# A two-layer mixer and expert kernel: the framework orders the engines' instructions by its time line simulation, and operands are put at equal places

## The chip, the core and the metric

The kernel runs on one core of a Trainium2 chip. The metric is the device time of one execution in microseconds. Five engines work side by side, each through its own list of instructions, strictly in the list's order: PE multiplies matrices (PEld is its loading of the stationary operand), DVE and ACT do elementwise work, POOL does small work and indirect DMAs, SP issues most of the DMAs. An instruction that has to wait for a semaphore holds up everything behind it on its engine.

## The reference

Two layers over 1,024 tokens of width 1,024 and 256 context tokens. In each layer:

```
h_x, h_c = modulate(x, ...), modulate(ctx, ...)          # layer norm, then scale and shift from w_mod
y_x, y_c = token_mixer(h_x, h_c, ...)                    # 4 mLSTM heads both ways and 4 attention heads, then w_out
x = post_norm(x, mx[2] * y_x, ln1_g, ln1_b)
x = post_norm(x, mx[5] * ec_moe(modulate(x, ...), w_router, w_gate, w_up, w_down), ln2_g, ln2_b)
```

`ec_moe` lets each of 16 experts take its 128 best tokens (32 of the context), multiplies them by `w_gate`, `w_up` and `w_down` (1024x1024 each) and adds the results back to their rows. Layer 0 does the same for the context; layer 1 has no context output.

## The kernel before

Float32 products are made from three fast matmuls (`mm3`, L83): an operand is split into a rounded part (`hi_act`, ACT, L90) and the rest (`lo_dve`, DVE, L93).

```
mm(ps, lh, rh, start=start, stop=False)     # L85: the first operand stays in the array,
mm(ps, lh, rl, start=False, stop=False)     # L86: the second streams through it
mm(ps, ll, rh, start=False, stop=stop)      # L87
```

The stages of a layer, with their time in layer 0 and layer 1 in the profile:

- Input (`phase_in`, L1492; 0 to 480 and 1795 to 2240 us). The normed and transposed input is held as `hTh0..2` and `hTl0..2` (`make_hT` L257, `border_hT` L289). Each of four mLSTM heads (`mlstm_head`, L551) projects K, V, Q and O (`p_block`, L339), convolves, and then goes through its chunks of 128 tokens: small matmuls that alternate with ACT, DVE and POOL. The transposed output of a head (`mlstm_out`, L664, whose transposes are L670 and read `hb`) is traced late, in the middle of the next head (`run_late`, L676), so that two streams lie side by side on PE: the next head's projections and this head's chunks.
- Attention (`latents` L681, `prep_kv` L790, `phase_mla` L809; 480 to 830 and 2240 to 2500 us).
- Output projection, norms, router (`phase_out`, L1006; 830 to 1040 and 2500 to 2640 us): ten tiles of 128 tokens in layer 0, eight in layer 1, each 48 matmuls of `omh`/`oml` with `woh`/`wol`; then the choice of tokens (`topk`, L1182), a serial chain on DVE.
- Experts (`phase_moe`, L1271; 1040 to 1795 and 2675 to 3245 us). `wsplit` (L1292) loads 512 KB of weights into a ring, splits it (`mhi`, `mlo`) and feeds PE: per expert 96 matmuls for gate and up (`A_ps`, operands `xTh`/`xTl`) and 48 for down (`B_ps`, operands `aTh`/`aTl`), each 128x512. Results are added to `zd` by indirect DMA (L1268). At the end of layer 0, layer 1 loads `w_in` (L336) and the rows of `zd` (`nz`, L1525).

What sets the order of the work: the Python code is traced in program order through a tile framework. When its context closes, the framework decides in which order the instructions of each engine stand in the program, places the tiles in SBUF and sets the semaphores. In the kernel before this order comes from a priority list: an earlier traced instruction has the higher priority, and a later one goes ahead of it where the framework takes the earlier one not to be ready yet. So the order isn't the traced one; for example the L670 transposes stand between the matmuls of a projection. One order is asked for by hand: the first four `lo_dve` of the experts stand behind the last row norm (L1301).

Tiles of a pool lie one behind the other in each partition, pools are stacked from the left and from the right. By the program's allocation, in bytes of a partition:

| matmuls | one operand | the other | apart, of 128 bytes |
|---|---|---|---|
| gate/up, both layers | xTh 131,040 | mhi 151,520 | 0 |
| down, layer 0 | aTh 64,832 | mhi 151,520 | 32 |
| down, layer 1 | aTh 47,520 | mhi 151,520 | 64 |
| output projection, layer 0 | omh 68,224 | woh 131,040 | 32 |
| output projection, layer 1 | omh 60,896 | woh 131,040 | 0 |
| scores (L763 to L767) | qh 45,728 | knh 128,992 | 64 |
| input, layer 0, `hTl0` with `whi` | hTl0 188,320 | whi 126,816 | 64 |

(`hTh2` and `hTl2` have 258 columns, 8,256 bytes, in layer 0, which is 64 more than a multiple of 128.) `hi` and `lo` parts lie alike.

Of the kernel before, what the change touches and what calls it, by code (L numbers as in the profile page):

```python
# [9 lines left out]
F32 = mybir.dt.float32  # L10
# [41 lines left out]
class Kern:  # L52
# [21 lines left out]
    def pool(self, es, name, bufs=1, space=None, side=None):  # L74
        kw = {"reuse_waits": "tile"}
        if space is not None:
            kw["space"] = space
        if side is not None:
            kw["side"] = side
        return es.enter_context(self.tc.tile_pool(name=name, bufs=bufs, **kw))  # L80


    def mm3(self, ps, lh, ll, rh, rl, start, stop):  # L83
# [173 lines left out]
    def make_hT(self, l, xrows, hp, p, psum, tag, ready, done):  # L257

        nc = self.nc
        cols = [n + 2 * (self.fold and g == 2) for g, (_, n) in enumerate(GROUPS)]  # L260
        self.hTh = [hp.tile([128, 8, n], F32R, name=f"hTh{g}") for g, n in enumerate(cols)]
        self.hTl = [hp.tile([128, 8, n], F32R, name=f"hTl{g}") for g, n in enumerate(cols)]

        def normed(i):
            xt = xrows(i)
            self.layer_norm_rows(xt, xt, 1e-6, p)
            return xt

        for g, (t0, n) in enumerate(GROUPS):
            hh, hl = self.hTh[g], self.hTl[g]  # L270
            xn = []
            for i in range(t0 // 128, (t0 + n) // 128):
                xn.append(normed(i))
                if g:
                    self.fill(self.nfill[0])
            if g == 0:
                ready()
            s = 1 if g == 2 else 0
            for kb in range(8):
                pt = psum.tile([128, 512], F32, name="pt", tag=tag)  # L280
                for i, xo in enumerate(xn):
                    nc.tensor.transpose(pt[:, i * 128:(i + 1) * 128], xo[:, kb * 128:(kb + 1) * 128], self.ident)
                sc = self.modc[l][:, s, 1, kb:kb + 1]
                nc.scalar.activation(hh[:, kb, :n], pt[:, :n], AF.Copy, scale=sc)
                nc.vector.scalar_tensor_tensor(hl[:, kb, :n], pt[:, :n], sc, hh[:, kb, :n].bitcast(F32), op0=OP.mult,
                                               op1=OP.subtract)
            done(g)
# [502 lines left out]
    def prep_kv(self, l, p2):  # L790

        nc, A = self.nc, self.A
        wkh = p2.tile([128, 2, 8, 128], F32R, name="wkh")
        wkl = p2.tile([128, 2, 8, 128], F32R, name="wkl")
        ckh = p2.tile([128, 2, TT], F32R, name="ckh")
        ckl = p2.tile([128, 2, TT], F32R, name="ckl")
        for kb in range(2):
            raw = p2.tile([128, 1024], F32, name="araw", tag="araw", bufs=1)
            nc.sync.dma_start(raw, A["w_ukv"][l, kb * 128:(kb + 1) * 128, :])
            rv = raw.rearrange("p (h w c) -> p w h c", h=4, w=2)  # L800
            hv = wkh[:, kb].rearrange("p (w h) c -> p w h c", w=2)
            lv = wkl[:, kb].rearrange("p (w h) c -> p w h c", w=2)
            for w in range(2):
                self.hi_act(hv[:, w], rv[:, w])
                self.lo_dve(lv[:, w], rv[:, w], hv[:, w])
        self.kv = p2, (wkh, wkl, ckh, ckl)
        yield from self.rms_norm_T(l, 1, 2, 55, (0, 1, 2), ckh, ckl, p2)

    def phase_mla(self, l, ctx_out, el):  # L809
# [3 lines left out]
        with ExitStack() as es:  # L813
# [49 lines left out]
                self.lo_dve(Vl[:, c, :], ps, Vh[:, c, :])  # L863
            el.close()
            pa = self.pool(es, f"aa{l}")
            rope = {}

            def project_q(ps, blk, t0, n):
# [84 lines left out]
            def stage(n, k):  # L953

                if n >= len(pairs):
                    return
                g, h, i0 = pairs[n]
                if k == 0 and i0 == 0:
                    if h % 2 == 0:
                        prep_rope(g, h // 2)  # L960
                    qs[g, h] = prep_q(g, h)
                elif k == 1:
                    ps_[n] = weights(g, h, i0, qs[g, h])
# [2 lines left out]
                stage(n, 0)  # L966
            for n in range(1):
                stage(n, 1)
            for n, (g, h, i0) in enumerate(pairs):
                stage(n + 2, 0)  # L970
                stage(n + 1, 1)
                if i0 == 0:
                    aos[g, h] = pa.tile([128, 512], F32, name="ao", tag="ao", bufs=2)
                ao = aos[g, h]
                values(g, h, i0, ps_.pop(n), ao)
                t0, nn = GROUPS[g]
                if i0 + 2 == nn // 128:
                    nc.scalar.dma_start(self.mixd[l][512 + h * 128:512 + (h + 1) * 128, t0:t0 + nn], ao[:, :nn])
# [27 lines left out]
    def phase_out(self, l, ctx_out, xsrc, es_keep):  # L1006
# [14 lines left out]
        self.sel = {}  # L1021
        with ExitStack() as es:
            p = self.pool(es, f"om{l}")
            n_tiles = NCH if ctx_out else NXC
            mixes = {}

# [244 lines left out]
    def phase_moe(self, l, ctx_out):  # L1271
# [2 lines left out]
        psum, tkp = self.psum, self.tkp  # L1274
        with ExitStack() as es:
            p = self.pool(es, f"mm{l}")
            md = self.modd[l]
            g5 = self.row(p, "g5", md[0:1, 5 * D:6 * D])
            if ctx_out:
# [359 lines left out]
```

## Time and profile before

| | us |
|---|---|
| three runs | 3304.8, 3297.15, 3305.44 |
| median | 3304.8 |
| the profiled execution: own time | 3297.7 |
| its span (first to last instruction) | 3295.6 |
| PE busy in the span | 3081.4 |
| DVE, ACT busy | 2373.5, 1790.0 |

How to read it: the views below are of that one profiled execution. Busy time of PE is not PE at its peak, as matmuls overlap; the distance from one start to the next tells the pace. "Idle before" names what ended a wait, and PEclk is the granted share of TensorE's clock, 1.0 for 2.4 GHz and 0.5 for 1.2 GHz.

### The profile page before, as it was taken

The numbers are of one execution on the slowest core, as the hardware profiler recorded it, in microseconds if no ns is written. First come the engines' busy times: TensorE is split into PE (matmuls) and PEld (weight loads), VectorE is DVE, ScalarE is ACT, GpSimd is POOL, SyncE is SP. The second block draws the span as 40 slices with busy tenths as digits, with TensorE's granted clock in tenths as the row PEclk, the third lists the DMA queues.
The fourth block names the chain that finished last, engine by engine and source line by source line (L and its number), as shares of the span: only waits on it lengthen the run. The fifth ranks groups of instructions, "written<-read, shape, count | busy, mean of one in ns | idle before, by whom it ended". The sixth has DMA issues, their size and how long they took to land.

```text
span 3295.6 us, 49911 instructions
## 1 busy us (share of the span) xinstructions
PE 3081.4 (94%) x18387; PEld 2405.8 (73%) x18387; DVE 2373.5 (72%) x4350; ACT 1790.0 (54%) x3057; POOL 392.7 (12%) x301
## 2 busy tenths in 40 slices
PE   7999999999998999999997799998998869999997
PEld 4667777788775777777775677786887758777775
DVE  5556655666677878777776676646776779999897
ACT  2323334455324666666664743334553358888786
POOL 0001001000010011011101201000000113343111
PEclk8999999999998999999999899999999979999999
DMA  6654213101658887788786332223015479999995
GB/s 229 200 161 120 66 63 90 37 25 61 226 198 311 303 291 281 291 300 293 285 297 208 108 89 77 65 85 80 20 39 195 144 273 383 384 376 383 355 359 180
DMA packets 259405, 653.82 MB, mean 198 GB/s; under 512 B 29430, under 2 KB 99128, under 8 KB 259160
## 3 DMA queue, kind: packets, MB, share of 16 engines
q1 hardware_dynamic: 234616, 581.03, 49.2%
q0 software_dynamic: 12592, 39.85, 5.0%
q10 hardware_dynamic: 11952, 29.76, 2.4%
q8 instruction: 144, 2.36, 0.3%
q14 instruction: 101, 0.83, 0.1%
HBM read 580.45 MB, written 62.75 MB: 195 GB/s over the span
## 4 chain that ended last, share of the span: by engine, by line
PE 60%; DVE 6%; DMA 3%; ACT 2%; issue 2%; POOL 1%; SPq 0%; POOLq 0%; ACTq 0%; DVEq 0%
PE A_ps L86 11%; PE A_ps L85 10%; PE A_ps L87 10%; PE C_ps L1328 5%; PE B_ps L86 3%; PE B_ps L87 3%; PE B_ps L85 3%; PE D_ps L1316 1%; PE C_ps L1122 1%; DMA E<-mxd 1%; PE B_ps L935 1%; DVE mlo L93 1%; PE D_ps L85 1%; PE B_ps L593 1%; PE D_ps L86 1%
## 5 line engine op out<-in xcount | busy, mean ns | idle before, releaser
L93 DVE TENSOR_TENSOR mlo<-mraw,mhi 128x1024 fp32r<-128x1024 f32 x768 | 911.2, 1221 | 148.5 <-ACT mhi L90 130.8
L90 ACT ACTIVATE mhi<-mraw 128x1024 fp32r<-128x1024 f32 x768 | 803.8, 1064 | 238.1 <-PE A_ps L87 148.0
L86 PE MATMUL A_ps<-mlo,xTh 128*128 128x512 f32 x1024 | 411.1, 401 | 7.8 <-DVE mlo L93 7.5
L87 PE MATMUL A_ps<-mhi,xTl 128*128 128x512 f32 x1024 | 404.2, 395 | 0.0
L85 PE MATMUL A_ps<-mhi,xTh 128*128 128x512 f32 x1024 | 396.0, 401 | 0.0
L85 PE MATMUL A_ps<-hTh,whi 128*128 128x512 f32 (+2 forms) x1032 | 375.6, 366 | 8.8 <-ACT hTh L90 5.1
L86 PE MATMUL A_ps<-hTl,whi 128*128 128x512 f32 (+2 forms) x1032 | 374.5, 363 | 1.5 <-DVE hTl L93 1.5
L87 PE MATMUL A_ps<-hTh,wlo 128*128 128x512 f32 (+2 forms) x1032 | 373.0, 362 | 0.5 <-DVE wlo L93 0.5
L86 PEld LDWEIGHTS A_ps<-mlo,xTh 128*128 128x128 f32 x1024 | 194.1, 190 | 54.5 <-DVE mlo L93 18.5
L85 PEld LDWEIGHTS A_ps<-hTh,whi 128*128 128x128 f32 x1032 | 199.7, 194 | 45.4 <-issue 9.6
L86 PEld LDWEIGHTS A_ps<-hTl,whi 128*128 128x128 f32 x1032 | 199.8, 194 | 37.6 <-issue 12.2
L85 PEld LDWEIGHTS A_ps<-mhi,xTh 128*128 128x128 f32 x1024 | 194.0, 190 | 44.5 <-issue 6.6
L87 PEld LDWEIGHTS A_ps<-hTh,wlo 128*128 128x128 f32 x1032 | 199.3, 193 | 30.2 <-issue 5.4
L87 PEld LDWEIGHTS A_ps<-mhi,xTl 128*128 128x128 f32 x1024 | 194.0, 189 | 37.1
L86 PE MATMUL B_ps<-mlo,aTh 128*128 128x512 f32 x512 | 203.7, 398 | 0.1
L87 PE MATMUL B_ps<-mhi,aTl 128*128 128x512 f32 x512 | 202.9, 396 | 0.0
L85 PE MATMUL B_ps<-mhi,aTh 128*128 128x512 f32 x512 | 200.5, 401 | 0.2 <-DVE mo L1427 0.2
L1268 POOL DMA_INDIRECT zd<-mo,idx x31 | 69.7, 2250 | 929.7 <-DVE mo L1427 864.1
L1264 POOL DMA_INDIRECT xg<-xn2d,idx x32 | 144.5, 4516 | 159.7 <-DVE oh L1237 49.0
L768 DVE TENSOR_REDUCE a_mx<-A_ps 128x1 f32<-128x512 f32 (+1 forms) x200 | 115.2, 589 | 60.0 <-PE A_ps L767 59.0
L90 ACT ACTIVATE PTh<-B_ps 128x512 fp32r<-128x512 f32 x164 | 94.3, 599 | 112.6 <-PE B_ps L935 110.7
L147 POOL TENSOR_TENSOR ln_rs<-rs_t,mhalf 128x1 f32<-128x1 f32 x56 | 48.2, 861 | 837.3 <-DVE rs_t L146 825.1
(442 smaller groups left out, 6280.1 us busy)
## 6 DMA issues: line engine op xcount, KB each, us to landing
mraw<-w_gate SPq DMA_DIRECT2D x256, 512.0 KB
mraw<-w_up SPq DMA_DIRECT2D x256, 512.0 KB
mraw<-w_down SPq DMA_DIRECT2D x256, 512.0 KB
wraw<-w_mod SPq DMA_DIRECT2D x56, 512.0 KB
wraw<-w_in SPq DMA_DIRECT2D x42, 512.0 KB
mraw<-w_mod SPq DMA_DIRECT2D x32, 512.0 KB
omx<-mixd SPq DMA_DIRECT2D x18, 512.0 KB
E<-mxd SPq DMA_DIRECT2D x32, 256.0 KB
```

The costliest lines, as they stand in the source:

```text
L85: mm(ps, lh, rh, start=start, stop=False)
L86: mm(ps, lh, rl, start=False, stop=False)
L87: mm(ps, ll, rh, start=False, stop=stop)
L90: self.nc.scalar.activation(hi, src, AF.Copy)
L93: self.nc.vector.tensor_tensor(lo, src, hi.bitcast(F32), op=OP.subtract)
L147: nc.gpsimd.tensor_tensor(out, t[:, :n], self.mhalf[:, :n], op=OP.pow)
L593: nc.tensor.matmul(dc[:, 129 * d:129 * d + 129], kw[:, d, :], vn[:, c, :], start=True, stop=True)
L768: nc.vector.tensor_reduce(mx[:, kj:kj + 1], s_[:, :kn], AX.X, OP.max)
L935: nc.tensor.transpose(pt[:, u * 256 + i * 128:u * 256 + (i + 1) * 128], Pt[:, kb * 128:(kb + 1) * 128], self.ident)
L1264: self.nc.gpsimd.indirect_dma_start(out=out, out_offset=None, in_=src, in_offset=bass.IndirectOffsetOnAxis(ap=idx[:, :1], axis=0))
L1268: self.nc.gpsimd.indirect_dma_start(out=dst, out_offset=bass.IndirectOffsetOnAxis(ap=idx[:, :1], axis=0), in_=src, in_offset=None, compute ...
L1328: nc.tensor.matmul(pc[32 * j:32 * j + 32, o:o + 256], lhsT, raw[:, j * 256:(j + 1) * 256], start=kb == 0, stop=kb == 7, skip_group_check=True)
```

## The change

The tile context is opened with `schedule_with_timeline_sim=True`: the framework now plays the program on its simulation of the chip's time line, with the engines, queues, semaphores and DMAs, and puts each engine's instructions in the order in which that simulation would take them. What is computed, the number of instructions that compute, and the traced program order stay. Besides, tiles that nobody reads are put into pools (`gap`), and the `hT` tiles are laid down in another order, so that what follows lies at another byte of its partition:

```diff
--- before.py
+++ after.py
@@ -78,6 +78,11 @@
         if side is not None:
             kw["side"] = side
         return es.enter_context(self.tc.tile_pool(name=name, bufs=bufs, **kw))
+
+    def gap(self, pool, n):
+
+        if n:
+            pool.tile([128, n // 4], F32, name="gap", tag=f"gap{n}")
 
 
     def mm3(self, ps, lh, ll, rh, rl, start, stop):
@@ -258,8 +263,10 @@
 
         nc = self.nc
         cols = [n + 2 * (self.fold and g == 2) for g, (_, n) in enumerate(GROUPS)]
-        self.hTh = [hp.tile([128, 8, n], F32R, name=f"hTh{g}") for g, n in enumerate(cols)]
-        self.hTl = [hp.tile([128, 8, n], F32R, name=f"hTl{g}") for g, n in enumerate(cols)]
+        t = {(a, g): hp.tile([128, 8, cols[g]], F32R, name=f"{a}{g}") for a, g in
+             (("hTh", 0), ("hTh", 1), ("hTl", 0), ("hTl", 1), ("hTh", 2), ("hTl", 2))}
+        self.hTh, self.hTl = ([t[a, g] for g in range(3)] for a in ("hTh", "hTl"))
+        self.gap(hp, 384)
 
         def normed(i):
             xt = xrows(i)
@@ -790,6 +797,7 @@
     def prep_kv(self, l, p2):
 
         nc, A = self.nc, self.A
+        self.gap(p2, 352)
         wkh = p2.tile([128, 2, 8, 128], F32R, name="wkh")
         wkl = p2.tile([128, 2, 8, 128], F32R, name="wkl")
         ckh = p2.tile([128, 2, TT], F32R, name="ckh")
@@ -863,6 +871,7 @@
                 self.lo_dve(Vl[:, c, :], ps, Vh[:, c, :])
             el.close()
             pa = self.pool(es, f"aa{l}")
+            self.gap(pa, 320)
             rope = {}
 
             def project_q(ps, blk, t0, n):
@@ -966,6 +975,7 @@
                 stage(n, 0)
             for n in range(1):
                 stage(n, 1)
+            self.gap(pa, 256)
             for n, (g, h, i0) in enumerate(pairs):
                 stage(n + 2, 0)
                 stage(n + 1, 1)
@@ -1021,6 +1031,7 @@
         self.sel = {}
         with ExitStack() as es:
             p = self.pool(es, f"om{l}")
+            self.gap(p, 288 if l == 0 else 0)
             n_tiles = NCH if ctx_out else NXC
             mixes = {}
 
@@ -1274,6 +1285,7 @@
         psum, tkp = self.psum, self.tkp
         with ExitStack() as es:
             p = self.pool(es, f"mm{l}")
+            self.gap(p, 160 if l == 0 else 64)
             md = self.modd[l]
             g5 = self.row(p, "g5", md[0:1, 5 * D:6 * D])
             if ctx_out:
@@ -1632,7 +1644,7 @@
     arrays = host_inputs(inputs)
     A = {k: nc.dram_tensor(k, v.shape, mybir.dt.from_np(v.dtype), kind="ExternalInput").ap() for k, v in arrays.items()}
     out = nc.dram_tensor("out", (1, T, D), F32, kind="ExternalOutput").ap()
-    with tile.TileContext(nc) as tc:
+    with tile.TileContext(nc, schedule_with_timeline_sim=True) as tc:
         Kern(tc, A, out).build()
     r = run_bass_kernel_spmd(nc, [arrays], core_ids=[0])
     return r.results[0]["out"]
```

By the sizes: in `phase_moe` 160 bytes move `aTh` of layer 0 to 64,992, and 64 bytes that of layer 1 to 47,584, both 0 apart from `mhi`; in `phase_out` 288 bytes bring `omh` of layer 0 from 32 to 64 apart; in `phase_mla` 320 bytes bring `qh` to 0 apart; in `make_hT` the new order brings `hTl0` and `hTl1` to 0 apart and leaves `hTl2` at 64.

## Rows read from the trace of the kernel before

**Rows 1.** The page, section 1: busy time (share of the span) and instructions.
```profile
span 3295.6 us, 49911 instructions
...
PE 3081.4 (94%) x18387; PEld 2405.8 (73%) x18387; DVE 2373.5 (72%) x4350; ACT 1790.0 (54%) x3057; POOL 392.7 (12%) x301
```

**Rows 2.** Windows by stage: stretch, its length, busy (count) by engine, clock, DMA, GB/s.
```profile
...
230.00:480.00 250.00, 237.15 (x1335) 191.26 (x1334) 151.67 (x355) 92.34 (x249) 20.33 (x41) 0.99 0.31 91
...
545.00:600.00 55.00, 44.37 (x196) 33.35 (x195) 35.23 (x64) 22.35 (x42) 1.92 (x3) 0.97 0.20 55
...
1040.00:1795.00 755.00, 750.99 (x5784) 544.75 (x5782) 582.75 (x851) 500.14 (x650) 82.12 (x49) 1.00 0.78 281
...
1830.00:2240.00 410.00, 388.94 (x2264) 327.45 (x2263) 253.31 (x553) 188.80 (x436) 43.54 (x69) 0.98 0.28 83
...
2540.00:2675.00 135.00, 96.94 (x549) 80.28 (x548) 97.37 (x251) 37.99 (x65) 16.60 (x17) 0.81 0.52 186
2675.00:3000.00 325.00, 324.59 (x1527) 259.08 (x1526) 311.43 (x418) 280.52 (x355) 111.94 (x18) 1.00 0.98 368
```

**Rows 3.** Waits of PE: line, releaser; us in total, times, longest.
```profile
...
PE B_ps L670 <- DVE hb L661: 25.1, 19, 2.7
PE B_ps L1190 <- DVE tkt L1179: 20.9, 2, 20.0
PE A_ps L311 <- ACT xo L180: 16.9, 2, 14.0
...
PE A_ps L85 <- ACT omh L90: 7.7, 2, 3.8
...
PE A_ps L87 <- DVE oml L93: 6.4, 4, 2.8
...
PE A_ps L85 <- ACT hTh L90: 5.1, 5, 1.2
...
PE A_ps L85 <- DVE knl L93: 4.5, 3, 2.6
```

**Rows 4.** Timeline of PE around 298 us: start, length, work [idle before <- releaser].
```profile
...
295.40 0.39 PE L87 MATMUL A_ps<-hTh,wlo 128*128 128x512 f32 x1
298.03 0.33 PE L670 MATMUL B_ps<-ident,hb 128*128 128x128 f32 x1 [2.24 <-DVE hb L661]
298.12 0.48 PE L85 MATMUL A_ps<-hTh,whi 128*128 128x512 f32 x1
```

**Rows 5.** Windows: two short stretches behind such waits.
```profile
...
296.00:304.00 8.00, 5.97 (x27) 5.24 (x28) 6.43 (x21) 1.78 (x5) 1.38 (x2) 0.79 0.20 59
464.00:473.00 9.00, 7.88 (x37) 6.53 (x38) 5.24 (x21) 2.43 (x9) 1.27 (x2) 0.81 0.14 49
```

**Rows 6.** Timeline of SP, layer 0 to layer 1 (start, length of the issue).
```profile
...
1799.35 4.13 SPq L336 DMA_DIRECT2D wraw<-w_in  x2
1803.52 1.27 SPq L371 DMA_DIRECT2D vrows<-conv_w  x1
...
1806.40 2.25 SPq L1525 DMA_DIRECT2D nz<-zd  x3
```

**Rows 7.** DMAs issued at 1785 to 1815 us; last number: us to landing.
```profile
...
zd<-mo,idx POOLq DMA_INDIRECT x1, 6.2
```

**Rows 8.** Timeline of POOL there.
```profile
...
1792.11 1.55 POOL L1268 DMA_INDIRECT zd<-mo,idx  x1 [10.12 <-DVE mo L1427]
```

**Rows 9.** Timeline of PE, layer 0 gate/up: first and last of 47 starts.
```profile
...
1085.64 0.40 PE L86 MATMUL A_ps<-mlo,xTh 128*128 128x512 f32 x1
...
1096.09 0.39 PE L87 MATMUL A_ps<-mhi,xTl 128*128 128x512 f32 x1
```

**Rows 10.** The same, layer 0 down projection: first and last of 47 starts.
```profile
...
1779.87 0.40 PE L86 MATMUL B_ps<-mlo,aTh 128*128 128x512 f32 x1
...
1790.64 0.40 PE L87 MATMUL B_ps<-mhi,aTl 128*128 128x512 f32 x1
```

**Rows 11.** The same, layer 1 down projection: first and last of 44 starts.
```profile
...
2726.04 0.39 PE L86 MATMUL B_ps<-mlo,aTh 128*128 128x512 f32 x1
...
2735.88 0.39 PE L87 MATMUL B_ps<-mhi,aTl 128*128 128x512 f32 x1
```

**Rows 12.** The same, layer 0 output projection: first and last of 54 starts.
```profile
...
844.10 0.39 PE L85 MATMUL A_ps<-woh,omh 128*128 128x512 f32 x1
...
856.47 0.39 PE L87 MATMUL A_ps<-woh,oml 128*128 128x512 f32 x1
```

## The prediction

> **What bounds the kernel now.** I read the page first, then the windows by stage, then what PE waits for, and last the timeline at the places that those waits name. The reader should see that PE is the bound: it is busy for 3081.4 of 3295.6 us [rows 1], so that all its idle time is 214 us, and no order of the instructions can take away more than that and the slow stretches that follow it. The stages differ. The experts of layer 0 leave PE 4 us of idle time in 755 [rows 2], so that order is worth nothing there and only the pace of a matmul counts. The experts of layer 1 have PE busy for 324.6 of 325 us, but the DMA engines are at 0.98 and DVE at 311 us in the same stretch [rows 2]: transfers stand right behind PE, and a faster matmul would wait for its weights. In the mLSTM stages (230 to 480 and 1830 to 2240 us) PE is busy for 0.949 of the time, around the start of attention for 0.81, and in the last tiles and the choice of tokens of layer 1 for 0.72, there at a granted clock of 0.81 [rows 2].
>
> What PE waits for is told by its waits [rows 3]. The largest sum is the transposes of a finished head, 25.1 us in 19 waits. The 20.9 us at L1190 are the serial choice of tokens on DVE, behind which PE has no other work of its own list; the 16.9 us at L311 are the way from the last expert of layer 0 through the norms to the first transposes of layer 1.
>
> **The order, part by part.** The change removes and adds no instruction that computes; it moves them, on every engine and on the DMA queues of SP, POOL and ACT. I do not know the new lists. I can say where the old list is bad, bound what a better or worse one gives there, and take a share.
>
> *Transposes of a head.* At 295.40 us the last projection matmul in front starts; the L670 transpose behind it starts at 298.03 after 2.24 us of idle time, and 0.09 us later a projection matmul runs that was ready all the time [rows 4]. That is an order made for a time line in which `hb` comes earlier than it does. PE also pays afterwards: in the 8 us from 296 the clock is 0.79, in 9 us at another such wait 0.81 [rows 5], which is 1.7 us lost each time (8 x 0.21, 9 x 0.19). If 8 of the 19 waits cost that, it is 14 us, and the whole is 39 us. An order by a closer time line puts projection matmuls in front and gains up to 39; one that errs the other way gains nothing or lets the chain of the next head start late, which is the second rival. I take a third, 13 us: the transposes free `oT` and the next head needs its place, so that they cannot come much later.
>
> *From layer 0 to layer 1.* The last `zd` scatter is issued at 1792.11 [rows 8] and lands 6.2 us later [rows 7], at 1798.3. SP issues the loads of those rows at 1806.40, behind two `w_in` loads that hold it for 4.13 us and the small `vrows` loads [rows 6]. So 8.1 us lie between, and they are on the path, as PE waits for the norms of these rows. Loads put in front gain up to 8.1; but then the `w_in` weights, which L85 needs next, are late by as much. I take half, 4 us. The other end is a loss of another 4.13 us for one more weight load in front.
>
> *Small waits where a stage begins.* `omh` 7.7, `oml` 6.4, `hTh` 5.1 and `knl` 4.5 us, 23.7 in all [rows 3]. Most of each is the latency of one chain with nothing else ready: between 0 and 23.7 I take 5. The other end is as much again, 5 us lost, where another list puts a second piece of work in front.
>
> *Choice of tokens.* The 20.9 us at L1190 stay: in layer 1 nothing else is left for PE. The order by hand (L1301) stays too, so the weight splits cannot go ahead of the last norm. Here 0, covered by nothing, and a loss only if DVE takes other work into the chain.
>
> *Experts.* 0 in both layers, for the reasons above. In layer 1 the cover is the DMA engines; if their share fell, PE would be the bound at the same length.
>
> The order gives 13 + 4 + 5 = 22 us; the ends are a gain of 39 + 8 + 24 = 71 and a loss that the second rival prices.
>
> **The places.** Starts of matmuls of one form, 128x512: in gate/up, with operands 0 apart, 47 starts take 10.45 us, 227.2 ns a step [rows 9]; in the down projection of layer 0, 32 apart, 10.77 us or 234.1 ns [rows 10]; in that of layer 1, 64 apart, 44 starts take 9.84 us or 228.8 ns [rows 11]; in the output projection of layer 0, 32 apart, 54 starts take 12.37 us or 233.4 ns [rows 12]. So 32 apart costs 6 to 7 ns and 64 apart 1.6. Layer 0 has 16 x 48 = 768 down matmuls: 768 x 6.9 = 5.3 us, on the path, as PE has no idle time there. Its output projection has 10 x 48 = 480 that go from 32 to 64 apart: 480 x 4.6 = 2.2 us. The scores (2 x 64 x 5 = 640 matmuls of 512 columns) and `hTl` of layer 0 go from 64 to 0: some 900 x 1.6 = 1.4 us, partly under waits, say 1. The down projection of layer 1 would gain 768 x 1.6 = 1.2 us and hides it under its DMAs. Together 8.5 us, between 0 (if something else in those stages sets the pace) and 10.
>
> A rule speaks against this term. The Trainium skill, "TensorE: Matmul & The Clock Gate", section "Step-by-step: what each phase is for", says that PE reads SBUF through two independent ports and that loading the next weights takes no bandwidth from the running matmul. By that rule the term would be 0. The steps of 227.2 and 234.1 ns differ between stages of the same form, both with PE busy; they do not agree with it as it stands, though no row isolates the place.
>
> **The sum.** 3297.7 - 22 - 8.5 = 3267.2 us against the profiled execution's own time. That execution stands 7 us under the median of the three runs, near the lowest of them; the new median may lie anywhere in the same scatter, so I add 5: **3272 us**, 1.0% under 3304.8.
>
> **The rivals.**
>
> 1. *Much more is won* (chance 0.12). All of the 71 us and the places: 3297.7 - 71 - 8.5 + 5 = 3223. For it speaks that every term comes from one cause, an order for a wrong time line; against it that chains have a latency that stays.
> 2. *The mLSTM stages get worse* (0.23; slower). PE has two streams there. An order that always fills PE with ready projection matmuls starts the small matmuls of a chunk later, the chain of a head drags behind, and at the last head of a layer no projection is left beside it. The price comes from the share of PE: these stages last 250 + 410 = 660 us at 0.949; where such a cover is missing it is 0.81 (545 to 600 us) [rows 2]. At 0.89, under halfway, they last 660 x (0.949/0.89 - 1) = 44 us longer: 3297.7 + 44 - 8.5 + 5 = 3338. It decides from a share of 0.907 on, where it eats 30 us. For it: an order is a greedy choice, and the old list was at least good enough for 0.949. Against it: PE's longest single waits there are under 3 us.
> 3. *The waits only change their names* (0.13), or the two lists turn out nearly the same, so that the change doesn't do what it says (0.04). Then the places alone remain: 3297.7 - 8.5 + 5 = 3294, at the bound of what can be told.
> 4. *The order helps and the places don't* (0.08): 3297.7 - 22 + 5 = 3281. This is what the rule on the two ports gives.
>
> **How the numbers follow.** The forecast has 0.40. About 0.3% (10 us) is what a measurement of this kernel can tell from no change, so "faster" is under 3295. The forecast, rivals 1 and 4 lie under it, 0.60, and about a third of rival 3 does, as does none of rival 2: 0.65, from which I take 0.03 for scatter of the forecast's unknown terms. Rival 3's rest and the near side of rival 2 are "same". The range goes from below rival 1's value, 3215, to that of rival 2, 3338; outside stay about 0.05 below and, as rival 2 has no end at 0.89, about 0.12 above. The forecast's own range, with a third of each gain more or less, is 3245 to 3292.
>
> **What would show it right or wrong.** Right: the waits of L670 for `hb` fall from 25.1 us to about 12 and the windows behind them are at a clock over 0.9; the `nz` loads are issued under 8 us after the scatter lands; the starts of down matmuls of layer 0 are 227 to 228 ns apart; the stage of the layer 0 experts is 5 us shorter. Rival 2 is right if PE's share in the mLSTM stages is under 0.907. Rival 3 if PE's idle time is again about 200 us with other names. Rival 4 if the down matmuls are still 234 ns apart. I would be wrong at the root if the experts of layer 1, which I leave as they are, change by more than 5 us: then the order of loads on SP or of splits on DVE matters there, and I have not priced it.

## Result: slower by 9.2%, and the profile after

| | before | after |
|---|---|---|
| median, us (6 runs each) | 3304.94 | 3605.39 |
| ratio, 95% interval | | 1.0921, 1.0909 to 1.0934 |
| profiled execution, span | 3295.6 | 3603.6 |

The prediction was 3272 us, and its range ended at 3338. The first reading is again the page's busy times, here of the kernel after, to be held against [rows 1]:

```profile
span 3603.6 us, 49960 instructions
PE 3179.0 (88%) x18387; PEld 2468.8 (69%) x18387; DVE 2369.3 (66%) x4350; ACT 1789.1 (50%) x3057; POOL 328.4 (9%) x301
```

The same 18,387 matmuls take PE 98 us more, and the span has 210 us more in which PE does nothing. DVE and ACT do their work in the same time. So two things went wrong: PE waits, and its work itself lasts longer.

To see where, I cut both spans at PE's own marks: the first matmul that reads `rn_q` (attention begins), `omh` (output projection), `xTh` (experts), the last context matmul of the experts, the first that reads `xo` (layer 1), and, behind the experts of layer 1, the last that reads `aTl`. Lengths in us:

| | input 0 | attention 0 | out, router 0 | experts 0 | between | input 1 | attention 1 | out, router 1 | experts 1 | end |
|---|---|---|---|---|---|---|---|---|---|---|
| before | 500 | 331 | 194 | 770 | 29 | 380 | 300 | 171 | 584 | 38 |
| after | 622 | 317 | 198 | 838 | 31 | 503 | 297 | 167 | 593 | 37 |

The two input stages lose 122 + 123 us, the experts of layer 0 lose 68, and the rest adds up to about -5. The windows of these three stages, first of the kernel before (stretch, its length, busy time with count of PE, PEld, DVE, ACT and POOL, granted clock, DMA share, GB/s):

```profile
0.00:500.00 500.00, 460.75 (x2531) 342.41 (x2532) 280.41 (x665) 164.98 (x404) 35.49 (x82) 0.97 0.45 140
...
1025.00:1795.00 770.00, 765.78 (x5839) 556.28 (x5838) 594.76 (x878) 512.44 (x667) 82.12 (x49) 0.99 0.78 283
...
1823.00:2203.00 380.00, 356.30 (x2095) 299.42 (x2095) 245.30 (x543) 181.64 (x425) 40.32 (x65) 0.97 0.26 79
```

and of the kernel after:

```profile
0.00:622.00 622.00, 499.60 (x2673) 380.99 (x2673) 279.95 (x666) 170.82 (x413) 41.37 (x86) 0.88 0.38 117
...
1137.00:1976.00 839.00, 821.66 (x5858) 550.91 (x5856) 586.91 (x879) 513.19 (x667) 85.94 (x49) 0.99 0.73 257
...
2006.00:2509.00 503.00, 406.95 (x2189) 350.07 (x2189) 248.08 (x539) 184.70 (x429) 40.26 (x69) 0.85 0.21 63
```

In the input stages PE's busy share falls from 0.92 and 0.94 to 0.80 and 0.81, and the clock from 0.97 to 0.88 and 0.85. In the experts PE is nearly as busy as before (0.98 of the time, 0.99 before) and at the same clock. Of the 69 us between these two windows 56 are busy time and 13 are waits: there it does the same matmuls in a more costly order.

**The input stages.** What PE waits for in the whole execution (line, releaser; us in total, times, longest), against 25.1 us for `hb` as the largest before [rows 3]:

```profile
PE D_ps L651 <- DVE hb L662: 61.9, 29, 5.4
PE B_ps L677 <- DVE hb L668: 37.4, 11, 9.0
...
PE B_ps L732 <- DVE rn_q L725: 26.6, 4, 12.7
PE B_ps L600 <- ACT kw L597: 19.1, 26, 1.4
```

The first line is new. A chunk's output matmuls (L651, L653) use one PSUM tile, which DVE frees when it has written `hb`. The timeline of PE after 212 us shows what these waits look like:

```profile
213.98 0.39 PE L653 MATMUL D_ps<-Cb,Wb 128*128 128x129 f32 x2
219.42 0.80 PE L651 MATMUL D_ps<-vn,E 128*128 128x129 f32 x2 [5.05 <-DVE hb L662]
...
225.78 0.80 PE L651 MATMUL D_ps<-vn,E 128*128 128x129 f32 x2 [4.28 <-DVE hb L662]
```

In this head there is no projection matmul between two chunks any more. Up to 213.75 us the projections of the next head ran (some 220 matmuls since 150 us, three blocks of 72), and the next one, of its fourth block, stands behind this head's last outputs and starts at 261.80 us. From 209 to 260 us PE is busy for 30.6 of 51 us at a clock of 0.73. By PE's lists, 34 of the 64 steps from one chunk's outputs to the next are like this, most of them in the first and last heads of layer 0 and the last of layer 1; before, none was without a projection matmul. In the other 30, mostly in the heads between, 7 to 43 stand there, and such a step takes some 7 us (median). In the stretch above, the projections were spent earlier, between the state matmuls of the chunks. For one chunk, first before (ACT's `kw`, then PE from the chunk's transposes to its state matmuls):

```profile
164.55 0.38 ACT L590 ACTIVATE kw<-B_ps,g_WS 128x128 f32<-128x128 f32 x1
...
163.66 0.27 PE L585 MATMUL B_ps<-ident,vT 128*128 128x128 f32 x1
...
165.66 0.38 PE L593 MATMUL B_ps<-vn,kw 128*128 128x129 f32 x2
```

then after:

```profile
156.56 0.62 ACT L597 ACTIVATE kw<-B_ps,g_WS 128x128 f32<-128x128 f32 x2
...
156.08 0.27 PE L592 MATMUL B_ps<-ident,vT 128*128 128x128 f32 x1
...
163.80 0.71 PE L600 MATMUL B_ps<-vn,kw 128*128 128x129 f32 x4
```

In both kernels ACT has `kw` ready 1.1 to 1.3 us after the start of the last transpose (at 164.93 and 157.18). Before, PE takes it 0.7 us later; after, 6.6 us later, because 21 projection matmuls and ten instructions of `w_mod` stand in front in its list. Over all 80 chunks the state matmuls start 0.03 us behind `kw` before and 2.14 us behind it after. By PE's lists, a chunk's transposes and its state matmuls have 3.8 projection matmuls between them on average before and 12.4 after. A head (from its first transposes to the next head's) takes 81.0 us before and 112.5 after, mean of six. Six times 31.5 us are 189 of the 245; the last heads, with nothing left beside them, lose 24 and 12, the start of layer 1 another 23, and the start of layer 0 gives 3 back.

**The experts of layer 0.** Groups of PE's instructions in this stage (busy us, mean ns | idle us before), before:

```profile
L1328 PE MATMUL C_ps<-mraw,xcT 128*32 128x256 f32 x2048 | 119.8, 381 | 0.0
...
L1328 PE MATMUL C_ps<-mraw,acT 128*32 128x256 f32 x1024 | 58.6, 380 | 0.0
```

and after:

```profile
L1340 PE MATMUL C_ps<-mraw,xcT 128*32 128x256 f32 x2048 | 143.6, 385 | 0.5 <-ACT xcT L999 0.5
...
L1340 PE MATMUL C_ps<-mraw,acT 128*32 128x256 f32 x1024 | 82.1, 384 | 0.0
```

The matmuls of the context rows need 47 us more, though one lasts as long as before. They are 32 columns wide and go to four column parts of the array; standing together, four start some 7 ns apart and run at once. Each leaves two instructions in the trace (1,024 of the first kind are called, 2,048 recorded). After, the timeline shows them torn apart:

```profile
1314.96 1.05 PE L1340 MATMUL C_ps<-mraw,xcT 128*32 128x256 f32 x10
...
1316.60 0.63 PE L1340 MATMUL C_ps<-mraw,xcT 128*32 128x256 f32 x6
...
1320.11 0.63 PE L1340 MATMUL C_ps<-mraw,xcT 128*32 128x256 f32 x4
...
1357.06 3.66 PE L1340 MATMUL C_ps<-mraw,xcT 128*32 128x256 f32 x64
```

From a group's first start to the next other matmul's, groups of 2, 4, 6 and 8 instructions, which are one to four matmuls, take 549, 556, 562 and 569 ns, and one of 64 takes 3592 ns (medians over the groups): in groups of four instructions, 64 would take 16 x 0.556 = 8.9 us. Before there were 53 groups, 44 of them of 64; after there are 165, 97 of them of 8 or fewer (the last group of the stage counted).

### The profile page after: what moved, and what is told of

The parts are those of the page before. It is cut to its first block, busy times and chain, and to the rows that moved or that the text cites. A ratio compares the mean times of both kernels' runs of the same rounds, so it can differ in the third digit from the quotient of the medians.

```text
span 3603.6 us, 49960 instructions
## 1 busy us (share of the span) xinstructions
PE 3179.0 (88%) x18387; PEld 2468.8 (69%) x18387; DVE 2369.3 (66%) x4350; ACT 1789.1 (50%) x3057; POOL 328.4 (9%) x301
## 4 chain that ended last, share of the span: by engine, by line
PE 71%; DVE 11%; DMA 6%; ACT 5%; issue 4%; POOL 1%; SPq 1%; ACTq 0%; POOLq 0%; DVEq 0%
PE A_ps L91 13%; PE A_ps L90 13%; PE A_ps L92 13%; PE C_ps L1340 5%; PE B_ps L91 3%; PE B_ps L90 3%; PE B_ps L92 2%; DVE mlo L98 2%; PE B_ps L944 2%; DMA Wb<-wtd 1%; PE C_ps L221 1%; PE D_ps L1328 1%; PE A_ps L770 1%; PE B_ps L600 1%; DMA mraw<-w_down 1%
## 5 line engine op out<-in xcount | busy, mean ns | idle before, releaser
L90 PE MATMUL A_ps<-hTh,whi 128*128 128x512 f32 (+2 forms) x1032 | 373.8, 366 | 20.1 <-ACT hTh L95 11.4
L90 PE MATMUL A_ps<-mhi,xTh 128*128 128x512 f32 x1024 | 341.5, 398 | 6.5 <-ACT mhi L95 3.5
L90 PE MATMUL B_ps<-mhi,aTh 128*128 128x512 f32 x512 | 171.7, 398 | 2.1 <-ACT mhi L95 1.7
L785 ACT ACTIVATE Pt<-A_ps,a_mx 128x512 f32<-128x512 f32 (+1 forms) x200 | 119.8, 612 | 54.0 <-DVE a_mx L782 48.0
L1340 PE MATMUL C_ps<-mraw,xcT 128*32 128x256 f32 x2048 | 143.6, 385 | 0.5 <-ACT xcT L999 0.5
L98 DVE TENSOR_TENSOR PTl<-B_ps,PTh 128x512 fp32r<-128x512 f32 x164 | 111.7, 685 | 41.6 <-ACT PTh L95 41.1
```

The source lines that it names most:

```text
L98: self.nc.vector.tensor_tensor(lo, src, hi.bitcast(F32), op=OP.subtract)
L785: nc.scalar.activation(Pt[:, k0:k0 + kn], sb[kj][:, :kn], AF.Exp, bias=mx[:, 4:5], scale=A_SCALE, accum_out=sm[:, kj:kj + 1])
L1340: nc.tensor.matmul(pc[32 * j:32 * j + 32, o:o + 256], lhsT, raw[:, j * 256:(j + 1) * 256], start=kb == 0, stop=kb == 7, skip_group_check=True)
```

## Experiments

All times are medians, compared with the kernel before on the same chip (its medians there 3299 to 3302 us); the ratio is to that, with its 95% interval.

**The order alone, the places alone.** Two kernels take the change apart.

```diff
     def gap(self, pool, n):
-        if n:
-            pool.tile([128, n // 4], F32, name="gap", tag=f"gap{n}")
+        return
...
-             (("hTh", 0), ("hTh", 1), ("hTl", 0), ("hTl", 1), ("hTh", 2), ("hTl", 2))}
+             (("hTh", 0), ("hTh", 1), ("hTh", 2), ("hTl", 0), ("hTl", 1), ("hTl", 2))}
```

> The changed kernel without its gaps and with the hT tiles in their old order, so only the order of the instructions differs from the kernel before. Theory A (the order alone costs the time; the places give back a little): 3608 to 3618 us, as the down projection and the output projection of layer 0 go back to 234 and 233 ns a matmul, 768 x 5.5 + 480 x 4.3 ns = 6.3 us, and the scores 1 to 2 us more. Rival B (the new places carry part of the loss): under 3590 us.

Measured: 3609.5 us, 1.0940 (1.0909 to 1.0971). Theory A. The other kernel:

```diff
-    with tile.TileContext(nc, schedule_with_timeline_sim=True) as tc:
+    with tile.TileContext(nc) as tc:
```

> The kernel before with the gaps and the new order of the hT tiles, and its old order of instructions. Theory A: 6 to 10 us under the kernel before, 3295 to 3299 us against 3305, with the down projection of layer 0 near 228.5 ns a matmul and the output projection near 229. Rival B (the places cost): over 3320 us. Third reading: within 3 us of the kernel before, if the shorter steps are hidden.

Measured: 3292.4 us, 0.9978 (0.9965 to 0.9991): 8 us won, as the places' term said. The starts of the down projection of layer 0 in this kernel, first and last of 47, and of the output projection, first and last of 54:

```profile
1773.55 0.40 PE L91 MATMUL B_ps<-mlo,aTh 128*128 128x512 f32 x1
...
1784.00 0.39 PE L92 MATMUL B_ps<-mhi,aTl 128*128 128x512 f32 x1
...
839.49 0.40 PE L90 MATMUL A_ps<-woh,omh 128*128 128x512 f32 x1
...
851.62 0.40 PE L92 MATMUL A_ps<-woh,oml 128*128 128x512 f32 x1
```

10.45 / 46 = 227.1 ns a step against 234.1 [rows 10], and 12.13 / 53 = 229.0 against 233.4 [rows 12]. As only places differ between these kernels, the place is now isolated: 0 apart 227, 64 apart 229, 32 apart 233 to 234 ns.

**One chain made tight by hand.**

```diff
+        with self.behind():     # tc.issue_after(the last state matmul of the head in front)
             if not early:
                 self.p_block(self.load_w_in(l, OFF_V + h * 128, wp), (0, 1, 2), evac_v, psum, "A")
             self.conv_silu(...)
             if not early:
                 self.p_block(self.load_w_in(l, OFF_O + h * 128, wp), qg, ...)
...
+            with self.behind():
                 self.latents(l, w, pk, pl, self.pool(el, f"ak{l}"), ps, ctx_out)
```

> The changed kernel, with the V, Q and O projections of the next head (and the latents behind the last head) put behind the last state matmul of a head by hand; only the K projection may still stand between the state matmuls. Theory A (the list puts some twenty projection matmuls into a round trip of PE and ACT that takes a quarter of that, so the state chain is stretched by about 72 x 2.1 = 151 us and uses up the projections that should cover the chunks' outputs): 150 to 230 us less, 3375 to 3455 us. Rival C (the stretched state is hidden; the single buffers of oT and the PSUM tile of the outputs set the pace of a head): less than 40 us won, over 3565 us. Rival D (the loads on SP come in a worse order): no change, 3600 to 3610 us.

Measured: 3611.9 us, 1.0944 (1.0914 to 1.0974). Theory A fell. The state chain did become tighter (2.84 us from chunk to chunk, against 3.95 in the kernel after and 1.85 before), but a head's outputs now take 78.0 us instead of 73.5, and a head 107.8 us. The projections had only moved: some 26 of them (the median by PE's list) now stood between two chunks' output matmuls, and 5 of the 64 steps were without any, not 34. With them the waits moved. The one of L651 (L655 here) for `hb` fell from 61.9 to 7.7 us, while PE now waits for `kw` for 55.6 us and not 19.1, as the state chain has lost its cover. And work off PE grew as a reason, from 8.1 us in the kernel after to 20.2 (the longest of these two waits is one in layer 0):

```profile
PE B_ps L604 <- ACT kw L601: 55.6, 64, 2.7
...
PE C_ps L643 <- DVE E L645: 20.2, 2, 11.0
```

In those 11 us, from 389.89 us, the loads of `E` and `Wb`, issued from 388.77 us on, landed, and POOL, ACT and DVE worked on them one after the other, DVE with other work in between. The time alone would fit rivals C and D as well. Against C stands that the wait for the outputs' PSUM tile nearly went and no time was won; against D the last step of the staircase below, where the lists of POOL and SP together carry only 24 us.

**The context matmuls kept together by hand.**

```diff
+                            with after(self.last_c):      # the last context matmul in front
                                 self.mm3(pg[hf], ...)
                     if ctx_out:
+                        with after(self.last_m):          # the last of the 48 matmuls in front
                             for k in range(8):
                                 col_tiled(pc, ...)
```

> The changed kernel, with the matmuls of the context rows in the layer 0 experts kept behind the 48 matmuls in front of them and ahead of the next 48, as they stand in the kernel before. Theory E (these matmuls run four at a time only while they stand together; 164 groups in place of 52 cost 41 us inside and 10 us at their edges): 50 to 70 us less, 3535 to 3555 us, and the stage back to about 775 us. Rival D (weights come late in this stage, DMA share 0.73 in place of 0.78): under 15 us won, over 3590 us.

Measured: 3579.2 us, 1.0840 (1.0808 to 1.0873), 26 us won: between the two theories. The stage fell from 838 to 808 us with 69 groups in place of 165. PE's busy time in it fell by 47 us, but PE now waited in it for 33 us instead of 17, mostly for the choice of tokens on DVE (`pk`, 17.0 us).

**Lists written out.** To see which engine's list carries the loss, I took the order of an engine from the kernel before and chained its instructions in the kernel after, so that the new way could order only the other engines. It makes their lists anew around the written one, so they are not the lists of the kernel after. Whatever is computed, the places and the flag stay.

```diff
+ORDERS = {'PE': ...}      # the place of each instruction in the list of the kernel before
...
+            tc.add_manual_dep(cur, prev.name, info, reason="order written out")   # issue order only
...
         Kern(tc, A, out).build()
+        pin(tc)
```

> The changed kernel, places and flag included, but PE's list is written out instruction by instruction as it stands in the kernel before; the lists of DVE, ACT, POOL and SP stay those of the new way. The state_tight run has shown that a tight state chain alone gives nothing. Theory F (PE's list alone carries the loss, by where it puts the small matmuls of the chunks and of the context rows): 3285 to 3315 us, as the kernel before with its places. Theory G (the lists of the other engines carry a good part, as DVE's results for PE stand behind work that waits for a DMA): over 3400 us.

Measured: 3513.8 us, 1.0648 (1.0624 to 1.0673). Theory G. The state chain is back at 1.98 us from chunk to chunk, the experts of layer 0 at 778 us; a head takes 93.2 us. PE still waits for `hb`:

```profile
PE B_ps L677 <- DVE hb L668: 42.8, 17, 4.5
PE D_ps L651 <- DVE hb L662: 25.7, 12, 4.8
```

and DVE's timeline beside one such wait (311.67 us, 3.90 us long) says why:

```profile
308.30 0.43 DVE L628 TENSOR_TENSOR E<-g_U,E 128x256 f32<-128x256 f32 x1 [2.94 <-DMA E<-mxd]
308.64 1.22 DVE L98 TENSOR_TENSOR wlo<-wraw,whi 128x1024 fp32r<-128x1024 f32 x1
309.78 0.62 DVE L635 TENSOR_TENSOR Wb<-qT,Wb 128x256 f32<-128x256 f32 x1
310.32 0.94 DVE L544 TENSOR_SCALAR cy<-praw,cols 128x1282 f32<-128x1282 f32 x1
311.18 0.34 DVE L662 SCALAR_TENSOR_TENSOR hb<-D_ps,h_dn,hb 128x128 f32<-128x128 f32 x1
```

ACT's half of `hb` was ready at 306.9. DVE's part of it, 0.34 us of work, stands behind a product that waits for a DMA and three other pieces.

The opposite, in the same way for DVE, ACT, POOL and SP with PE left free:

> The opposite: the lists of DVE, ACT, POOL and SP written out as in the kernel before, and PE's list left to the new way, which now orders PE beside those lists. Theory F: 3580 to 3630 us, as the changed kernel. Theory G: under 3500 us. If both this run and the one with PE's list written out come near the kernel before, any one of the lists is enough to hold the others, and the loss needs all of them.

Measured: 3776.1 us, 1.1428 (1.1403 to 1.1454): worse than with all lists new, which neither theory had. PE's free list beside four foreign ones is worse than five that were made together. Two parts of PE's list, by a mark on the stage that traced the instruction:

```diff
+    @staged
     def phase_in(self, ...):          # in the other kernel: phase_moe
...
+            if cur.name not in STAGE:
+                continue
```

> The changed kernel, with PE's list written out as in the kernel before for the instructions of the input stage (both layers) alone. Theory F: the 122 + 123 us that the two input stages lost come back, 3605 - 245 = 3360 us, give or take 20. Theory G: less than half of that, over 3480 us.

Measured: 3494.4 us, 1.0588 (1.0562 to 1.0615). Theory G, 111 us won: the input stages gave back 138 of their 245 us (622 to 551, 503 to 436), and attention took 22 of these (317 to 331, 297 to 306).

> The changed kernel, with PE's list written out as in the kernel before for the instructions of the experts (both layers) alone. Theory E (context matmuls torn apart): the 69 us of layer 0 come back and some of the 9 us of layer 1, 3605 - 72 = 3533 us, give or take 12; the groups of context matmuls are 52 again and not 164. Rival: the waits at the start of the stage, which took back 16 us when the groups were kept together by hand, take them here as well, 3570 to 3585 us.

Measured: 3550.6 us, 1.0758 (1.0733 to 1.0782), 55 us won. Theory E in its stage: 838 to 777 us, and the context matmuls are back to their old busy times:

```profile
L1353 PE MATMUL C_ps<-mraw,xcT 128*32 128x256 f32 x2048 | 119.8, 381 | 0.0
L1353 PE MATMUL C_ps<-mraw,acT 128*32 128x256 f32 x1024 | 58.6, 380 | 0.0
```

The experts of layer 1 took 6 us of it back. So here PE's list carries 61 of the 68 us: its busy time is back (763 us), and waits of 14 us are left. In the input stages it carries only a part.

**The staircase.** DVE's list added, then ACT's, then all, by the same edit with more keys in `ORDERS`.

> The changed kernel with the lists of PE and DVE written out as in the kernel before; ACT, POOL and SP stay new. With PE's list alone 3514 us were measured, with PE waiting for DVE's hb 68 us in 29 waits, where the convolution's passes of 1.5 us and loads that had not landed stood in front of hb on DVE. Theory G1 (DVE's list carries the rest): 3290 to 3350 us, and the waits for hb back at 25 to 30 us. Theory G2 (the issue of the E and Wb loads on SP, or ACT's list, carries the rest): over 3430 us.

Measured: 3364.4 us, 1.0195 (1.0174 to 1.0217): between the two theories, nearer G1. PE's waits for `hb` are back:

```profile
PE B_ps L677 <- DVE hb L668: 26.0, 19, 2.5
PE D_ps L651 <- DVE hb L662: 4.0, 4, 1.1
```

> The lists of PE, DVE and ACT written out as in the kernel before; POOL and SP stay new. Theory G1: 3285 to 3310 us, hardly less than with PE and DVE alone. Theory G2 with ACT: 3285 to 3310 us, but much less than with PE and DVE alone. Theory G2 with SP's loads: over 3380 us.

Measured: 3320.1 us, 1.0067 (1.0050 to 1.0084). 44 us more, 14 of them in the experts of layer 1 (596 to 582), where I had priced any loss at nothing. With PE's and DVE's lists old, ACT's new list carries this loss; but it isn't the only one that can, as the kernel below with ACT's list old and DVE's new takes 599 us there.

> A control: all five lists written out as in the kernel before, places new, flag on. The same as the kernel before with its places, 3285 to 3299 us (3292 measured there). Anything above 3310 us would say that the writing out itself, or the semaphores that the new way sets, costs time, and the runs with written-out lists would have to be read anew.

Measured: 3296.5 us, 0.9994 (0.9980 to 1.0008), as expected: the writing out costs nothing that shows, and POOL's and SP's lists carry the last 24 us. Period of a head down the stairs: 112.5, 93.2 (PE), 82.6 (DVE), 81.3 (ACT), 80.9 (all).

**Is the new way better anywhere?** Its attention stage of layer 0 looked 13 us shorter.

```diff
+    @staged
     def phase_in(self, ...):
...
+    @staged
     def phase_moe(self, ...):
```

> All five lists written out as in the kernel before for the input stages and the experts; attention, output projection and router stay with the new way, whose attention stage of layer 0 lasted 317 us against 330 before and whose layer 1 stages from attention to router 464 against 471. If these gains are real, 3292 - 13 - 7 = 3272 us, give or take 8, under both kernels. Rival (the stage's first mark only moved, because work from it was done earlier beside idle PE): 3290 to 3320 us.

Measured: 3301.3 us, 1.0005 (0.9992 to 1.0018). The rival: attention of layer 0 lasts 331 us, as before. The 13 us were work done earlier beside an idle PE.

**One new list among four old ones.**

> The lists of PE, ACT, POOL and SP written out as in the kernel before, and DVE's list left to the new way, which now orders DVE beside four old lists. If a new list does harm by itself: 3380 to 3460 us, near the 3297 us of five old lists plus the 149 us that DVE's list took off in the staircase. If the new lists only do harm together: under 3340 us.

Measured: 3440.0 us, 1.0442 (1.0416 to 1.0468): DVE's new list does harm by itself. A head takes 90.1 us. Two kernels then wrote out, of DVE's list, only the order of the chunk results and one other kind of work among themselves (the diff is the set of lines, as traced in the kernel before):

```diff
+chain = {651, 652, 655, 656, 657, 661}                  # h_dn, hb and its statistics
+dve_conv: chain | {537, 539, 542, 544}                  # the passes of the convolution
+dve_loads: chain | {621, 628}                           # the products that need E and Wb
```

> PE, ACT, POOL and SP written out as in the kernel before; on DVE only the chunk results (h_dn, hb and their statistics) and the convolution's passes stand in the order of the kernel before among themselves, the rest of DVE's list is new. If passes of 1.5 us in front of the chunk results hold the heads up: 40 to 66 us less than 3440 us, 3374 to 3400 us, with the period of a head back from 90 to 82 us. If the products that wait for the loads of E and Wb do it: under 20 us less, over 3420 us.

Measured: 3427.8 us, 1.0375 (1.0353 to 1.0397), 12 us won, a head 88.7 us.

> The same with the products of E and Wb in place of the convolution's passes. If these, which wait for a DMA ahead of a finished chunk, hold the heads up: 3374 to 3400 us and a period of 82 us. If the convolution does: over 3420 us. If each does half, both runs lie near 3407 us.

Measured: 3412.4 us, 1.0344 (1.0324 to 1.0364), 28 us won, a head 85.2 us, the input stages 510 + 402 us: 34 of their 66 us. So products that wait for a DMA ahead of finished chunks are about half of it and the convolution a small part, less than either text expected of its cause. What the rest is was not tried.

**The prediction's own moves.** The old way, PE's and SP's lists written out with two moves.

```diff
 # in PE's list of the kernel before
-o4 P2 h1 P1 h1 P1 h1 P1 h1 P11      (o: outputs, P: projection, h: L670 transposes)
+o4 P10 h1 P1 h1 P1 h1 P1 h1 P3
 # in SP's list
-w_in x2, vrows x5, nz x3
+nz x3, w_in x2, vrows x5
```

> No flag; the kernel before with its places, its lists of PE and SP written out with two moves: each L670 transpose of a finished head (L677 here) stands 8 projection matmuls, 1.8 us, later (less where a matmul into the same PSUM tiles comes first), and the first three loads of zd stand ahead of the two w_in loads and the small vrows loads. If the prediction's steps hold: 13 us from the transposes (their waits fall from 25 us to under 12) and 4 us from the loads (issued at most 2 us after the scatter lands, the boundary of the layers 4 us shorter), 3292 - 17 = 3275 us, give or take 7. Rival (the wait comes back elsewhere, as the O projection of the next head waits for the transposes' single buffer): 3287 to 3297 us. Rival (the delay lengthens the loop of the heads): over 3300 us.

Measured: 3303.0 us, 1.0015 (1.0005 to 1.0025): slower than the places alone (3292.4). What PE waits for in it:

```profile
PE D_ps L651 <- DVE hb L662: 18.7, 11, 3.3
PE B_ps L384 <- DMA vrows<-conv_b: 18.3, 1, 18.3
...
PE A_ps L318 <- ACT xo L185: 12.7, 3, 7.3
```

The transposes' own wait fell to 1.7 us, but 18.7 us of the first line are new. The loads of `zd` were issued 1.2 us after the scatter landed, not 8.3, and layer 1's first transposes came 3 us sooner; then they went on slower (`xo`, and `hf` behind it, were late), and the first chunk of layer 1 started 145.8 us after the experts' last context matmul, not 136.7 as with the places alone. No moved transpose lies in that stretch, so these 9 us are the price of the loads' move; in the next kernel, which moves transposes but leaves the loads, it is 137 us again.

> The same with the transposes 4 projection matmuls (0.9 us) later and the loads of zd left where they were. If the step on the transposes holds: half to all of 13 us, 3280 to 3286 us. Rival: 3288 to 3297 us.

Measured: 3289.0 us, 0.9974 (0.9963 to 0.9985). That is not told apart from the places alone (0.9965 to 0.9991): the rival. By the ratios the difference is 1 us, give or take some 6 (an estimate from both intervals), so a gain of 13 is out. The wait for the transposes fell from 25.0 to 10.5 us, and 5.9 us came back at L651. It is the fastest kernel seen here, with all that it owes to the places.

## Why the prediction was wrong, step by step

- **That the new order comes nearer to the chip** carried the forecast's 22 us of gain, and no row stood behind it. It failed: the order alone cost 309 us. The list for the changed kernel leaves 12.4 projection matmuls' room for an answer of ACT that arrives 1.1 us after the question. Why the framework's time line leaves that room was not looked into; that the lists do is shown, on PE by `kw` and on DVE by `hb`.
- **The transposes, 13 us.** The wait was real, and the way to take it away (more projections in front) was right: 25 to 10.5 us, then to 1.7. The gain wasn't: the time came back as a wait for the next chunk. The changed kernel didn't take the step either; its wait there is 37.4 us.
- **The layer boundary, 4 us.** Moved by hand, it won 3 us at its place and had lost 9 in all by the first chunk. I had named the other end (late weights, a loss of 4) and taken the wrong one. The changed kernel left two `w_in` loads in front, 6.6 us between landing and issue (1981.0 to 1987.6). That meets the sign that the text had named (under 8 us), but the way from the last context matmul to layer 1's first transposes still grew from 28.7 to 30.7 us.
- **Small waits, 5 us, and the choice of tokens, 0.** `omh` grew from 7.7 to 16.2 us, `hTh` from 5.1 to 11.4, while `oml` fell from 6.4 to 1.8; the wait for the choice of tokens went from 20.9 to 28.1.
- **Experts 0.** This is the worst step of the reasoning. Idle time of 4 us in 755 bounds what an order can win there, not what it can lose: 68 us were lost with the same instructions in a worse order, at an unchanged clock, 56 of them as longer busy time. And layer 1, called safe behind its DMAs, lost 9 us. The text's own test for being wrong at the root (over 5 us there) was met.
- **The places, 8.5 us.** Right as a sum: 8 us measured alone (3 to 12 by the interval). How it divides isn't shown: between the two profiled executions the experts of layer 0 are 3.7 us shorter (5.3 were expected), the stage of the output projection is 3 us longer (2.2 less were expected), and the input of layer 0 is 6 us shorter (499.7 to 493.5), which it isn't in the kernel with the same places and all lists written out (499.5). The row now speaks for itself, as [rows 10] and the new starts differ in the place alone. The Trainium skill, "TensorE: Matmul & The Clock Gate", section "Step-by-step: what each phase is for", says that the two read ports are independent; a pace that goes from 234.1 to 227.1 ns with the operands' distance does not agree with it, and rival 4, which followed it, is out.
- **Rival 2** had PE's part of the mechanism and its order of events nearly word for word: ready projections in front, chunks that drag, nothing left beside the last head. DVE's part, finished chunks behind other work, stood in none of the rivals, and PE's list written out gave back only 138 of the 245 us. Its price, 44 us, was less than a fifth of the 245. I put the share of PE at 0.89 "under halfway" for no reason in the rows; it went to 0.80 and 0.81, the value of the uncovered stretch in [rows 2]. And I priced share alone: 660 x (0.949/0.81 - 1) = 113 us. The clock fell with the share, to 0.88 and 0.85. Share times clock went from 0.92 x 0.97 to 0.80 x 0.88 and from 0.94 x 0.97 to 0.81 x 0.85, factors of 1.26 and 1.32, which give 632 and 502 us; measured are 622 and 503. (These are the shares and clocks of the kernel after: they account for the loss and would not have foretold it.) [Rows 5] had shown the clock, and the first term used it; the rival did not.

What stays open: how the loss of the input stages divides among the lists. The staircase (92, 149, 44 and 24 us) is one order of many, and mixed lists cost time of their own: PE's list alone written out made attention 38 us longer in layer 0 (317 to 356), and four of five written out took 3776 us. Shown is that PE's list written out takes away 61 of the 68 us that the experts of layer 0 lost, that PE's and DVE's together take away most of the input stages' loss (209 of 245 us), and that all five together give the old time.

## What to carry to other kernels

A busy engine bounds what a new order can win, not what it can lose: before a list is replaced as a whole, name for each stage what the old one keeps together (matmuls that run at once, a chain's next link in front of ready work) and price it broken, share times clock. A chain through several in-order engines needs its links at the front of every list it passes, so mending one list can move the wait to the next, as it did here; written-out lists, one engine at a time, show where it goes. Two edits that share a change are best run apart: here 8 us were won under a loss of 309.

## What the runs showed of the hardware

- A matmul with 32 stationary columns is nearly free beside three others to the other column parts, and costs a whole pass alone: groups of 2 to 8 instructions (one to four matmuls) take 549 to 569 ns, one of 64 takes 3592. The Trainium skill, "TensorE: Matmul & The Clock Gate", section "Part 3: Packing small matmuls — row/col tiling", says that such matmuls run concurrently in one array; the trace agrees, and adds that two other matmuls between them, the fewest that stand there, are enough to end it.
- The pace of a 128x512 matmul depends on how far its two operands lie apart within 128 bytes of a partition: 227, 229 and 233 to 234 ns at 0, 64 and 32.
- Where chunks ran without cover, PE lost twice: from 560 to 622 us it was busy for 24.9 of 62 us at a granted clock of 0.53, close to the lower of its two levels.
